# Two blocks in fp32 from split operands: new durations in the estimate that paces background steps, and two operand splits half a chunk earlier

## The chip, the cores and the metric

The kernel runs on one core of a Trainium2 chip. The metric is the time of one execution on the device in microseconds (us); "the median" is that over several executions.

## The reference

Two blocks follow each other on 256 tokens of 2048 features, in fp32. Cut to what matters here:

```python
# block 1
h = x @ w_in                                   # all inputs of four branches, and their gates
y_a = pool_mixer(...) * silu(a_gate);  y_b = spatial_gating(...) * silu(b_gate)
y_c = sliding_window_attention(...) * silu(c_gate);  y_d = conformer_conv(...) * silu(d_gate)
x = layer_norm(ALPHA * x + sum(sigmoid(g[i]) * (y[i] @ w_branch[i])) @ w_out)
# block 2
z, xbc, dt, q, k, v, f = split(rmsnorm(x) @ w_in_2)
y_ssd = rms(ssd(conv(xbc), dt) * silu(z))      # in two groups g of 512 features
y_fox = softmax(q k' / 8 + cum(f) - cum(f)') v # 16 heads of 64: "fox", causal
x = x + concat(y_ssd, y_fox) @ w_out_2
x = x + peer(rmsnorm(x))                       # top-k of keys, then 16384 experts: u, gelu, v
return rmsnorm(x)
```

## The kernel before, in words

**Stream.** Every weight passes through one stream of chunks of 128x2048 fp32 (1 MB, `load`, three buffers `wr`), and each chunk is worked in two halves. `split` (lines 283 to 303) makes of a half two fp32r operands: ACT casts `wh` from `wr` (a CAST), then DVE subtracts to give `wl`. TensorE multiplies three times per tile of 128 features: hi by hi, lo by hi, hi by lo; a half chunk is 24 matmuls of 256 columns (`T_chunk`) or 12 of 512 (`N_chunk`). There are four pairs of split buffers, and `split` is called three halves ahead (`LOOK`): the cast of half h+3 writes to the buffer that half h-1 used. Half chunks are counted from 0 below: the queries and keys of block 2 are halves 430 to 461 (one query or key tile of 128 features is two halves), its `z` 462 to 477, its `w_out_2` starts at 478.

**Background steps.** Everything between the large products (normalizations, both attentions, the SSD) is written as generators, "steps", in four lanes (`Tasks`, lines 62 to 160). After the third tile of each half chunk `bg()` calls `tasks.tick()`, which issues steps while the estimated clocks of DVE and ACT are less than 5 us ahead of PE's (`room`). The clocks are kept by `charge` from `Meter.cost` (lines 171 to 190), which is an estimate of each instruction's length: it decides nothing but which step is issued after which half chunk, that is, the order of the instructions on each engine. All PE, DVE and ACT instructions pass through `Meter` and so carry line 208.

**Where the order is forced.** `tasks.until` and `tasks.require` (lines 121 to 150) issue the steps of a named task at once, with no work of the stream between them. `ev_q2(j)` (line 1203) takes query tile j out of PSUM; there are two buffers for queries, so it first runs fox j-2 up to its last use of query j-2 (`until`). `pre_wout2` (line 1316) stands ahead of half 478: it evacuates `z`, requires fox 4 to 7, and casts and subtracts the fox outputs into XH and XL (`split_y`). `pre_yn(g)` (line 1329) requires the normalization of group g of the SSD for both token halves (`yn{g}0`, `yn{g}1`) and splits its result into XH and XL. At line 1344 a pair in place of one function names the first and the second half of a chunk.

A step of fox, of one block of 128 queries: two products K by q, scale and mask (DVE), row maximum; *then* two exponentials (ACT); *then* a reciprocal and two scalings (DVE); *then* transposes (PE, `bg<-cst,LS`) and a copy (ACT, `LS<-bg`); *then* the product with V (PE, `bg<-LS,VN`) and a copy to YF (ACT).

```python
def room(self):
    c = self.clock
    return max(c["dve"], c["act"]) < c["pe"] + HORIZON
def charge(self, eng, cost):
    lag = 0.0 if c.eng is None else 0.25 if c.eng != eng else 0.125 if eng == "dve" else 0.0
    t = max(self.clock[eng], c.t + lag) + cost
```

Of the kernel before, what the change touches and what calls it, by code (L numbers as in the profile page):

```python
# [7 lines left out]
FR = mybir.dt.float32r  # L8
U32 = mybir.dt.uint32
BF = mybir.dt.bfloat16  # L10
# [53 lines left out]
class Tasks:  # L64
# [83 lines left out]
    def charge(self, eng, cost):  # L148
        c = self.cur
        lag = 0.0 if c.eng is None else 0.25 if c.eng != eng else 0.125 if eng == "dve" else 0.0  # L150
        t = max(self.clock[eng], c.t + lag) + cost
        self.clock[eng] = t
        if c is not self.main:
            c.t, c.eng = t, eng


def size(ap):
    n = 1
    for d in ap.shape[1:]:
        n *= d  # L160
    return n
# [5 lines left out]
class Meter:  # L167
# [3 lines left out]
    def cost(self, name, out, a, k):  # L171
        n = size(out)
        if self.which == "pe":
            if name == "transpose":
                return n * 2 / 2400
            return n * (1 if a[1].dtype in (FR, BF) else 4) / 2400
        if self.which == "act":
            c = 0.04 + 0.89e-3 * n + (0.09 if k.get("accum_out") is not None else 0.0)
            f = TABLES.get(a[1]) if name == "activation" else None
            if f and f != self.tasks.table:  # L180
                self.tasks.table = f
                c += 1.28
            return c
        if name in ("bn_stats", "tensor_reduce", "max", "max_index"):
            n = size(a[-1 if name == "max_index" else 0])
        if name == "tensor_scalar" and not (hasattr(a[1], "shape") and hasattr(a[2], "shape")):
            return 0.1 + 0.6e-3 * n
        if name == "tensor_copy":
            return 0.1 + 0.6e-3 * n
        return (0.13 if name == "scalar_tensor_tensor" else 0.08) + 1.04e-3 * n  # L190

    def plain(self, name, out, a):
        n = size(out)
# [18 lines left out]
def kern(tc, A, out):  # L212
    nc = tc.nc
    with ExitStack() as ctx:
        ctx.enter_context(tc.manual_schedule())
        _kern(tc, nc, ctx, A, out)


def _kern(tc, nc, ctx, A, out):
    tasks = Tasks(4)  # L220
# [44 lines left out]
    def add_chunks(src, idxs, fns, cols=D, pres=None):  # L265
        for n, i in enumerate(idxs):
            stream.append((src[i], cols, fns[n], pres[n] if pres else None))
# [3 lines left out]
    def load(c):  # L271
        if c >= len(stream):
            return
        src, cols, _, _ = stream[c]
        t = wraw.tile([P, D], F32, name="wr")
        if c:
            nc.sync.dma_start(t[:, :cols], src)
        else:
            nc.sync.dma_start(t[:, :HALF], src[:, :HALF])
            load_x(1)  # L280
            nc.sync.dma_start(t[:, HALF:], src[:, HALF:])
        raws[c] = t

    def split(hc, eng=None):
        c, half = divmod(hc, 2)
        if c >= len(stream):
            return
        n = stream[c][1] // 2
        r = raws[c][:, half * n:half * n + n]
        h = wspl.tile([P, HALF], FR, name="wh")  # L290
        l = wspl.tile([P, HALF], FR, name="wl")
        SC.copy(h[:, :n], r)
        if stream[c][2] is state.get("dtf"):
            r, l = [x.rearrange("p (k n) -> p k n", k=8) for x in (r, h)]
            V.tensor_sub(l[:, :, 32:64], r[:, :, 32:64], l[:, :, :32].bitcast(F32))
        else:
            (eng or V).tensor_sub(l[:, :n], r, h[:, :n].bitcast(F32))
        splits[hc] = (h, l, max(tasks.clock["dve"], tasks.clock["act"]))
        if half:
            load(c + RAW_BUFS)  # L300
# [93 lines left out]
    def catch(upto, eng=None):  # L394
        while state["next"] <= upto:
            split(state["next"], eng)
            state["next"] += 1
# [923 lines left out]
    def split_y(g0, g1):  # L1321
        YS, YF = b2["YS"], b2["YF"]
        for g in range(g0, g1, 2):
            s = slice(g, g + 2)
            y = YS[:, s] if g < 8 else YF[:, g - 8:g - 6]
            SC.copy(XH[:, s], y)
            V.tensor_sub(XL[:, s], y, XH[:, s].bitcast(F32))

    def pre_yn(g):
        def f():  # L1330
            tasks.require(f"yn{g}0", f"yn{g}1")
            split_y(4 * g, 4 * g + 4)
        return f

    def ev_wout2(n):
        def f(t, ps):
            s = slice(n * 512, (n + 1) * 512)
            V.tensor_tensor(X[t][:, s], X[t][:, s], ps, op=OP.add)
            junk = b2["w"].tile([P, 512], F32, name="t2")
            SC.activation(junk, X[t][:, s], AF.Square, accum_out=small[:, 16 + 4 * t + n:17 + 4 * t + n])  # L1340
        return f

    evs = [ev_wout2(n) for n in range(4)]
    for n, kq, pre in [(0, 0, pre_wout2), (0, 1, (None, pre_yn(0))), (0, 2, None), (1, 0, None), (1, 1, None),
                       (1, 2, (None, pre_yn(1))), (0, 3, None), (1, 3, None)]:
        add_chunks(A["w_out2"], [4 * n + kq], [N_chunk(kq, evs[n], (2, 3, 0, 1), slot=n)], pres=[pre])
    for n in (2, 3):
        add_chunks(A["w_out2"], range(4 * n, 4 * n + 4),
# [348 lines left out]
    for hc in range(2 * len(stream)):  # L1697
        c, half = divmod(hc, 2)
# [4 lines left out]
        pre = stream[c][3]  # L1703
        if not isinstance(pre, tuple):
            pre = (pre, None)
# [126 lines left out]
```

## Time and profile before

| | us |
|---|---|
| three runs | 3096.13, 3102.93, 3100.11 |
| their median | 3100.11 |
| the profiled execution, its own time | 3101.19 |
| its span in the profile | 3099.5 |
| mean granted TensorE clock of it | 0.995 |

The profiled execution is 1.08 us above the median, and 1.7 us of its time lie around the span. The table of engines on the page gives busy time and its share of the span, then the number of instructions; PEld is the loading of weights into TensorE, which runs beside the matmuls. The granted clock is a share of full speed (1.00 is 2.4 GHz, 0.50 is 1.2 GHz). A row of the timeline gives start and length in us, engine, line, operation, output<-input and how many were merged; what stands in brackets is the idle time ahead of it and who ended it.

### The profile page before, as it was taken

The numbers are of one execution on the slowest core, as the hardware profiler recorded it, in microseconds if no ns is written. First come the engines' busy times: TensorE is split into PE (matmuls) and PEld (weight loads), VectorE is DVE, ScalarE is ACT, GpSimd is POOL, SyncE is SP. The second block draws the span as 40 slices with busy tenths as digits, with TensorE's granted clock in tenths as the row PEclk, the third lists the DMA queues.
The fourth block names the chain that finished last, engine by engine and source line by source line (L and its number), as shares of the span: only waits on it lengthen the run. The fifth ranks groups of instructions, "written<-read, shape, count | busy, mean of one in ns | idle before, by whom it ended". The sixth has DMA issues, their size and how long they took to land.

```text
span 3099.5 us, 53098 instructions
## 1 busy us (share of the span) xinstructions
PE 3053.1 (99%) x21964; PEld 2850.0 (92%) x21964; DVE 2200.7 (71%) x3195; ACT 1575.3 (51%) x2199; POOL 223.6 (7%) x187
## 2 busy tenths in 40 slices
PE   8999999999999989999999999999999999999998
PEld 8899999999999869897899999999999888888887
DVE  8899866555555567766489989788796666666665
ACT  4443565444444445556454457667675444444444
POOL 0000000000000020100000003233130000000000
PEclk9999999999999989999999999999999999999999
DMA  7555555555555535433545655666658766666654
GB/s 274 184 198 198 179 187 187 197 190 203 182 201 191 186 127 181 173 132 131 201 150 188 221 207 202 258 244 220 257 199 327 278 239 228 250 245 248 241 216 150
DMA packets 92226, 640.61 MB, mean 207 GB/s; under 512 B 10272, under 2 KB 10448, under 8 KB 17744
## 3 DMA queue, kind: packets, MB, share of 16 engines
q1 hardware_dynamic: 78192, 559.06, 49.9%
q0 software_dynamic: 13504, 77.63, 6.9%
q8 instruction: 172, 2.82, 0.4%
q14 instruction: 70, 0.57, 0.1%
q10 hardware_dynamic: 288, 0.52, 0.0%
HBM read 601.53 MB, written 35.65 MB: 206 GB/s over the span
## 4 chain that ended last, share of the span: by engine, by line
PE 96%; DVE 1%; ACT 1%; issue 1%; POOL 0%; DMA 0%; DVEq 0%; SPq 0%; ACTq 0%
PE pm L208 92%; PE bg L208 4%; ACT wh L208 1%; DVE wl L208 0%; DVE X L208 0%; DVE XL L208 0%; POOL keys L1516 0%; DMA wr<-w_in 0%; DVE stg L208 0%; ACT XH L208 0%; DVE gb L208 0%; DVE PX L208 0%; ACT PX L208 0%; ACT keys L208 0%; POOL Ad L1567 0%
## 5 line engine op out<-in xcount | busy, mean ns | idle before, releaser
L208 DVE TENSOR_TENSOR wl<-wr,wh 128x1024 fp32r<-128x1024 f32 x1048 | 1293.9, 1237 | 824.1 <-ACT wh L208 818.9
L208 ACT CAST wh<-wr 128x1024 fp32r<-128x1024 f32 x1054 | 1108.8, 1053 | 1383.5 <-PE pm L208 1325.8
L208 PE MATMUL pm<-XH,wh 128*128 128x256 f32 x4976 | 1393.7, 280 | 8.0 <-ACT wh L208 8.0
L208 PE MATMUL pm<-XL,wh 128*128 128x256 f32 x4976 | 1383.8, 278 | 0.0
L208 PE MATMUL pm<-XH,wl 128*128 128x256 f32 x4960 | 1380.4, 278 | 0.5 <-DVE wl L208 0.5
L208 PEld LDWEIGHTS pm<-XH,wh 128*128 128x128 f32 x4976 | 941.9, 189 | 14.1 <-ACT wh L208 8.0
L208 PEld LDWEIGHTS pm<-XL,wh 128*128 128x128 f32 x4976 | 937.5, 188 | 1.0 <-issue 0.7
L208 PEld LDWEIGHTS pm<-XH,wl 128*128 128x128 f32 x4960 | 932.7, 188 | 0.9 <-DVE wl L208 0.8
L208 PE MATMUL pm<-wh,whl 128*128 128x512 f32 x1024 | 398.3, 389 | 0.0
L208 PE MATMUL pm<-wh,whh 128*128 128x512 f32 x1024 | 398.3, 389 | 0.0
L208 PE MATMUL pm<-wl,whh 128*128 128x512 f32 x1024 | 398.3, 389 | 0.0
L208 PEld LDWEIGHTS pm<-wl,whh 128*128 128x128 f32 x1024 | 192.2, 188 | 39.9
L208 PEld LDWEIGHTS pm<-wh,whh 128*128 128x128 f32 x1024 | 192.2, 188 | 39.9
L208 PEld LDWEIGHTS pm<-wh,whl 128*128 128x128 f32 x1024 | 192.2, 188 | 39.8
L208 PE MATMUL pm<-wh,XH 128*128 128x512 f32 x448 | 179.5, 401 | 3.7 <-ACT XH L208 3.7
L208 PE MATMUL pm<-wh,XL 128*128 128x512 f32 x448 | 177.1, 395 | 0.7 <-DVE XL L208 0.7
L208 PE MATMUL pm<-wl,XH 128*128 128x512 f32 x448 | 177.7, 397 | 0.0
L1516 POOL TENSOR_TENSOR keys<-cst,t 128x512 f32<-128x512 f32 x64 | 137.1, 2142 | 207.1 <-ACT ga L208 206.9
L208 PE MATMUL pm<-YH,wh 128*128 128x256 f32 x512 | 144.1, 281 | 0.0
L208 PE MATMUL pm<-YL,wh 128*128 128x256 f32 x512 | 143.7, 281 | 0.0
L208 PE MATMUL pm<-YH,wl 128*128 128x256 f32 x512 | 143.7, 281 | 0.0
L208 DVE SCALAR_TENSOR_TENSOR CV<-R,par,CV 128x256 f32<-128x256 f32 x240 | 117.0, 487 | 7.3
(288 smaller groups left out, 2368.2 us busy)
## 6 DMA issues: line engine op xcount, KB each, us to landing
wr<-w_in SPq DMA_DIRECT2D x190, 1024.0 KB, 4.8
wr<-uT SPq DMA_DIRECT2D x128, 1024.0 KB, 4.9
wr<-v SPq DMA_DIRECT2D x128, 1024.0 KB, 4.9
wr<-w_branch SPq DMA_DIRECT2D x32, 1024.0 KB, 4.8
wr<-w_out SPq DMA_DIRECT2D x32, 1024.0 KB, 4.8
wr<-wq SPq DMA_DIRECT2D x16, 1024.0 KB, 4.8
Ad<-ast POOLq DMA_DIRECT2D x16, 1024.0 KB, 5.1
Gd<-stg POOLq DMA_DIRECT2D x16, 1024.0 KB, 11.8
```

Source lines behind the costliest of these rows:

```text
L208: return f(out, *a, **k)
L1516: G.tensor_tensor(x, it, t3[:, 0, n0:n0 + 4, None].to_broadcast([P, 4, P]), op=OP.subtract)
```

## The change

Two things. `Meter.cost` gets other constants (a matmul column 1/16 longer, ACT and DVE operations longer by 0.02 to 0.08 us and by 2 to 12% per element, accumulation on ACT 0.2 in place of 0.09), and in `split` DVE's subtraction is charged from ACT's clock + 0.25 on, where before it was charged as if it waited for nothing. And `pre_yn(0)` and `pre_yn(1)` stand ahead of the first half of their chunks (halves 480 and 488) where they stood ahead of the second.

```diff
-            return n * (1 if a[1].dtype in (FR, BF) else 4) / 2400
+            return n * (17 / 16 if a[1].dtype in (FR, BF) else 4) / 2400
         if self.which == "act":
-            c = 0.04 + 0.89e-3 * n + (0.09 if k.get("accum_out") is not None else 0.0)
+            c = 0.12 + 0.91e-3 * n + (0.2 if k.get("accum_out") is not None else 0.0)
...
         if name == "tensor_scalar" and not (hasattr(a[1], "shape") and hasattr(a[2], "shape")):
-            return 0.1 + 0.6e-3 * n
+            return 0.14 + 0.67e-3 * n
         if name == "tensor_copy":
-            return 0.1 + 0.6e-3 * n
-        return (0.13 if name == "scalar_tensor_tensor" else 0.08) + 1.04e-3 * n
+            return 0.14 + 0.67e-3 * n
+        return (0.15 if name == "scalar_tensor_tensor" else 0.1) + 1.1e-3 * n
...
+        at = tasks.main.t
         SC.copy(h[:, :n], r)
+        tasks.main.t = max(at, tasks.clock["act"] + 0.25)
...
             (eng or V).tensor_sub(l[:, :n], r, h[:, :n].bitcast(F32))
+        tasks.main.t = at
...
-    for n, kq, pre in [(0, 0, pre_wout2), (0, 1, (None, pre_yn(0))), (0, 2, None), (1, 0, None), (1, 1, None),
-                       (1, 2, (None, pre_yn(1))), (0, 3, None), (1, 3, None)]:
+    for n, kq, pre in [(0, 0, pre_wout2), (0, 1, pre_yn(0)), (0, 2, None), (1, 0, None), (1, 1, None),
+                       (1, 2, pre_yn(1)), (0, 3, None), (1, 3, None)]:
```

No instruction is added or removed. The order differs in halves 4 to 190 (block 1's projections) and 400 to 489 (block 2 up to its w_out_2); from half 490 on it is as before. Three places, in the rows of the instructions' order (names: `pm`, `bg` PSUM tiles, the number tells one tile from another; LS the scores of fox in two lanes; VN the values; t a sigmoid's output; xN merges equal instructions).

PE where query 2 of block 2 is evacuated, between halves 447 and 448, before:

```order
L208 MATMUL pm<-XL,wh 128x256
L208 MATMUL pm<-XH,wl 128x256
L208 MATMUL bg_14584<-K_12613,q_14208 128x256
L208 MATMUL pm<-K_12613,q_14208 128x256
L208 MATMUL pm<-XH,wh 128x256
```

and now:

```order
L208 MATMUL pm<-XL,wh 128x256
L208 MATMUL pm<-XH,wl 128x256
L208 MATMUL bg_14529<-cst,LS_12603 128x128 x2
L208 MATMUL bg_14533<-LS_12603,VN 64x128 x2
L208 MATMUL bg_14537<-K_12613,q_14184 128x256
L208 MATMUL pm<-K_12613,q_14184 128x256
L208 MATMUL pm<-XH,wh 128x256
```

The whole second part of fox 2's first block (transposes, product with V) and the K by q of its second block now stand between two matmuls of the stream, where only the K by q did. The same holds ahead of halves 452, 456 (fox 3, fox 4) and, without the exponentials, 460 (fox 5).

DVE at the same place, now:

```order
L208 TENSOR_SCALAR smf_14494<-smf_14494 128x2
L208 TENSOR_TENSOR PX<-PX,bg_14497 128x256
L208 TENSOR_TENSOR wl<-wr,wh 128x1024
L208 RECIPROCAL smf_14494<-smf_14494 128x2
L208 TENSOR_SCALAR LS_12603<-LS_12603,smf_14494 128x128 x2
```

The reciprocal and the scalings that those transposes read stand behind the `wl` of half 451, issued just ahead of them.

ACT at the start of w_out_2, ahead of half 478, now:

```order
L208 CAST wh<-wr 128x1024 x2
L208 ACT_TABLE_LOAD
L208 ACTIVATE t_15645<-pm 128x512
L208 ACTIVATE t_15648<-pm 128x512
L208 COPY LS_12603<-bg_15651 128x512
L208 COPY YF<-bg_15666 128x128
L208 ACT_TABLE_LOAD
L208 ACTIVATE LS_12604,smf_15663<-LS_12604,smf_15663 128x256 x2
L208 COPY LS_12604<-bg_15677 128x512
L208 COPY YF<-bg_15683 128x128
L208 CAST XH<-YF 128x512 x2
```

Before, the same `t` (sigmoids of z) were followed at once by `CAST XH<-YF`: fox 6 and fox 7 were done but for fox 7's last product with V. Now 3 steps of fox 6 and 6 of fox 7 are issued here with no matmul of the stream between them on PE.

ACT further on, from there to the splits of `pre_yn(0)`, before:

```order
L208 CAST XH<-YF 128x512 x2
L208 ACTIVATE PX,ss_15719<-PX 128x512
L208 ACT_TABLE_LOAD
L208 ACTIVATE ss_15719<-ss_15719,eps_81 128x1
L208 CAST wh<-wr 128x1024
L208 ACTIVATE PX,ss_15739<-PX 128x512
L208 ACTIVATE ss_15739<-ss_15739,eps_81 128x1
L208 CAST wh<-wr 128x1024 x2
L208 CAST XH<-XS 128x512 x2
```

and now:

```order
L208 CAST wh<-wr 128x1024 x2
L208 ACTIVATE XS<-bg_15748,par 128x128 x4
L208 CAST XH<-XS 128x512 x2
L208 CAST wh<-wr 128x1024
L208 ACTIVATE XS<-bg_15784,par 128x128 x4
```

`CAST XH<-XS` is the split of `pre_yn(0)`. It now stands half a chunk sooner, and the scaling of `yn01` (`XS<-bg_15748,par`) is forced right ahead of it.

## Rows read from the trace of the kernel before

**Rows 1.** The page: busy time, share of the span, instructions of each engine.

```profile
PE 3053.1 (99%) x21964; PEld 2850.0 (92%) x21964; DVE 2200.7 (71%) x3195; ACT 1575.3 (51%) x2199; POOL 223.6 (7%) x187
```

**Rows 2.** The page: share of each engine in the chain that ended last.

```profile
PE 96%; DVE 1%; ACT 1%; issue 1%; POOL 0%; DMA 0%; DVEq 0%; SPq 0%; ACTq 0%
```

**Rows 3.** PE's waits: who waited for whom: us in total, times, longest.

```profile
PE bg L208 <- issue: 9.5, 1, 9.5
PE pm L208 <- ACT wh L208: 8.0, 1, 8.0
PE bg L208 <- DVE diag L208: 7.2, 2, 5.0
```

**Rows 4.** Waits of all engines, the same columns.

```profile
ACT wh L208 <- PE pm L208: 1325.8, 910, 4.5
```

**Rows 5.** Chain that ended last: start, length, what, number of instructions.

```profile
208.31 8.48 PE pm L208 x72
217.24 8.18 PE pm L208 x72
...
512.49 617.34 PE pm L208 x4863
```

**Rows 6.** ACT and DVE timeline in the queries and keys of block 2.

```profile
1303.21 1.05 ACT L208 CAST wh<-wr 128x1024 fp32r<-128x1024 f32 x1 [2.00 <-PE pm L208]
...
1304.29 1.22 DVE L208 TENSOR_TENSOR wl<-wr,wh 128x1024 fp32r<-128x1024 f32 x1 [0.79 <-ACT wh L208]
...
1305.67 0.37 ACT L208 COPY LS<-bg 128x256 f32<-128x256 f32 x1 [1.14 <-PE bg L208]
```

**Rows 7.** DVE timeline at the end of z.

```profile
1448.30 0.16 DVE L208 RECIPROCAL smf<-smf 128x2 f32<-128x2 f32 x1
1448.49 0.62 DVE L208 TENSOR_SCALAR LS<-LS,smf 128x256 f32<-128x256 f32 x2
```

**Rows 8.** PE timeline at the end of z and in w_out_2: start, length.

```profile
1430.21 0.48 PE L208 MATMUL bg<-K,q 64*128 64x256 f32 x1
...
1441.38 0.99 PE L208 MATMUL bg<-cst,PX 128*128 128x128 f32 x4 [2.02 <-DVE PX L208]
...
1449.39 0.60 PE L208 MATMUL bg<-cst,LS 128*128 128x128 f32 x4
...
1470.27 0.79 PE L208 MATMUL pm<-wh,XH 128*128 128x512 f32 x1 [3.66 <-ACT XH L208]
1471.80 0.80 PE L208 MATMUL pm<-wh,XL 128*128 128x512 f32 x1 [0.74 <-DVE XL L208]
```

**Rows 9.** Stretches: us; PE, PEld, DVE, ACT, POOL busy (instructions); granted clock; DMA share; GB/s.

```profile
1347.00:1353.00 6.00, 5.11 (x48) 4.75 (x47) 5.12 (x12) 4.70 (x13) 1.43 (x2) 1.00 0.34 145
...
1441.00:1445.00 4.00, 3.62 (x11) 3.07 (x12) 1.46 (x2) 2.75 (x9) 0.00 (x0) 0.57 0.02 2
1469.00:1476.00 7.00, 4.99 (x12) 3.63 (x13) 5.60 (x9) 2.69 (x4) 0.00 (x0) 0.53 0.54 171
```

**Rows 10.** ACT timeline, end of z and w_out_2.

```profile
1432.67 0.25 ACT L208 COPY YF<-bg 128x128 f32<-128x128 f32 x1
...
1438.35 1.03 ACT L208 CAST wh<-wr 128x1024 fp32r<-128x1024 f32 x1
1439.40 1.28 ACT L208 ACT_TABLE_LOAD   x1
1440.69 0.51 ACT L208 ACTIVATE LS<-LS,smf 128x256 f32<-128x256 f32 x1
...
1451.24 0.60 ACT L208 COPY LS<-bg 128x512 f32<-128x512 f32 x1
...
1457.85 1.09 ACT L208 ACTIVATE t<-pm 128x512 f32<-128x512 f32 x2
...
1467.72 1.98 ACT L208 CAST wh<-wr 128x1024 fp32r<-128x1024 f32 x2
1469.60 1.13 ACT L208 CAST XH<-XS 128x512 fp32r<-128x512 f32 x2
```

## The prediction, made before the changed kernel ran

> **What bounds the kernel now.** I read the share of each engine first, then the chain that ended last, then PE's waits, then the timeline where the order changes. PE is busy 99% of the span, DVE 71% and ACT 51% [rows 1], and the chain that ended last is PE for 96% [rows 2]: the stream of matmuls sets the time, and a change in the order can gain only where PE waits. The three largest waits, 9.5, 8.0 and 7.2 us, are at the start of the program and at the boundary of the blocks [rows 3]; the change does not touch what they wait for. The cover of all background work is therefore nearly complete already. What gives it is the distance between split and use: ACT's casts wait 1325.8 us in total for PE to leave a buffer [rows 4], so each cast starts as soon as PE ends a half chunk, and PE has two more halves ready.
>
> PE itself has two speeds at the same granted clock. In the chain, 72 matmuls of the stream (three halves) take 8.48 us or 8.18 us, 117.8 or 113.6 ns each, and the pieces on either side of one group of background matmuls can differ so [rows 5]. The piece from 512.49 us on took 617.34 us for 4863 matmuls, of which 384 have 512 columns (the 32 half chunks of w_out, 12 each) and count double: 5247 units of 256 columns, 117.7 ns each. So the longest piece without background matmuls ran at the slower of the two [rows 5].
>
> **The change part by part.** No instruction is added or removed, and the longer estimates cost nothing by themselves. They make `room` close earlier, so that steps come later in the stream. That matters where a step is demanded at a fixed place: what is not done by then is issued there at once, with PE's stream behind it.
>
> *Four chains at the queries, halves 448, 452, 456, 460.* The order shows one step there before and five, five, five and four now: exponentials, reciprocal and scalings, transposes and copy, product with V, K by q. In front of them stand the cast and the subtraction of the half that is split at the same place. That cast can start only when PE is through with the half before [rows 4], so the chain starts when PE has nothing left: cast 1.05, `wl` 1.22, which covers the exponentials beside it, copy 0.37 [rows 6], reciprocal 0.16 and two scalings 0.62, taken from ones of 256 columns [rows 7]. The matmuls in it only move, so PE's idle time is 1.05 + 1.22 + 0.16 + 0.62 + 0.37 = 3.4 us in each. It sits between two matmuls of the stream, and nothing covers it.
>
> An idle PE can cost more after it. Where PE waited 2.02 us for PX [rows 8], the granted clock of the 4 us that follow was 0.57, between the levels of 2.4 GHz (1.00) and 1.2 GHz (0.50), with PE busy 3.62 us [rows 9]: 3.62 x 0.43 = 1.6 us lost. In 1347 to 1353 us PE idled 0.9 us in sum (6.00 less 5.11), and the clock stayed at 1.00 [rows 9]. A wait of 3.4 us is nearer the first, so I take 1.6 after each; the bounds are 0 and 2.3, the loss after a wait of 3.66 us: 4.99 busy us in 1469 to 1476 us at 0.53, 4.99 x 0.47 [rows 8, 9]. Four chains: 4 x (3.4 + 1.6) = +20.0; from 4 x 3.4 = 13.6 to 4 x (3.4 + 1.05 for another cast ahead + 2.3) = 27.
>
> *The chain ahead of w_out_2, half 478.* Nine steps of fox 6 and 7 are issued there. Off PE it holds one cast 1.05, a table load 1.28, two sigmoids 1.09, a copy of 512 columns 0.60, one to YF 0.25, a second table load 1.28 (the next function is an exponential), two exponentials of 0.51, [rows 10], reciprocal and scalings 0.78 [rows 7] and a copy 0.60: 7.95 us. Beside it PE does the first transposes, 0.60, and the K by q, 0.48 [rows 8]: 7.95 - 1.08 = 6.9 us idle. With 1.6 for the clock +8.5; bounds 6.9 and 10.2 (a further cast and 2.3).
>
> What a change of function costs is a row here: the cast before one ended at 1439.38, the load took 1.28 us and the exponential began at 1440.69 [rows 10], so nothing is drained around it. The Trainium skill, page "ScalarE: Activation LUTs", section "Table sets: the hidden batching unit", gives some 2.7 us for each load, drain included; by it two loads would make 2.8 us more, and the time 3123. The row speaks against it, and the sum goes by the row.
>
> *`pre_yn(0)` half a chunk sooner, half 480.* It forces two steps of `yn01`, transposes and scaling, which before had a half chunk, 2.7 us (a third of 8.18), of cover. The wait that I can compare is the one for the same XH at half 482, 3.66 us [rows 8]; the bounds are 0 and 3.7, and I take 1.5, since the products with the new XH come only half 482 and a half chunk of the stream lies between. For `pre_yn(1)` the normalization is done long before; nothing.
>
> *What is gained.* In before, XH for group 0 of the SSD is cast at 1469.60, behind two casts of the stream that begin at 1467.72 [rows 10]; PE waits 3.66 us for it and 0.74 for XL [rows 8], and loses 2.3 to the clock as above. Half a chunk sooner the split stands ahead of those casts. The 2.02 us at 1441.38, for PX, with its 1.6, falls as well, since those steps move. Together -(3.66 + 0.74 + 2.02 + 2.3 + 1.6) = -10.3; at the least -6.4, if the clock gives nothing.
>
> *POOL, SP and the DMAs.* A load is issued with the split of a second half, at the same place as before; POOL's mask sums move with their steps and are not in any of the chains. The halves 4 to 190 are reordered too: there DVE is the busiest beside PE, and I put 0 with 4 us to either side for pieces that change between the two speeds of PE.
>
> **Sum.** 20.0 + 8.5 + 1.5 - 10.3 = +19.7 us on the profiled execution's 3101.2: 3120.9. That execution is 1.1 us above the median of the runs, so 3120 against 3100.11. With the bounds of each term the forecast alone gives 3110 to 3130.
>
> **The rivals.** *(a) The same waits, but the long stretch at the faster speed.* Background matmuls of block 1 come later now, and the stretch without any starts some 500 matmuls later, after other groups. Which speed holds after the last group, the rows do not tell: it changes at some groups and not at others [rows 5]. At the fast speed the 4359 matmuls that remain (4743 units) gain 4743 x (117.7 - 113.6) = 19.4 us: 3120 - 19 = 3100. For it: both speeds are common. Against: before had the slow one there. It is decided by the length of a half chunk after 570 us. [...]
>
> *(b) Faster.* The waits at 1441 and 1470 us go, and the forced chains are hidden. This decides if PE still holds matmuls of the stream when the chain's cast begins; from a chain start 2.5 us earlier on, the four would cost under 1 us each and the whole under the 10.3 that is won. Time: 3100.1 - 10.3 = 3090. Against it: the cast waits for PE's last matmul of the half [rows 4], so there is nothing left to hide behind.
>
> *(c) The pacing moves nothing that counts*, since what PE waits for is set elsewhere [rows 3]: 3100 to 3101. Against it: the order shows the chains with no matmul between.
>
> *(d) Worse than the sum:* each chain also delays the casts behind it, so that PE waits for `wh` once more after each, another 1.05 for six places, and the slower speed spreads to 190 to 570 us (some 3300 units x 4.1 ns, 13 us at most): about 3140.
>
> **How the numbers follow.** A measurement of this kernel can tell 0.2%, 6.2 us, from no change: below 3093.9 is faster, above 3106.3 slower. Forecast 0.50, (a) 0.32, (b) 0.08, (c) 0.05, (d) 0.05. Slower: the forecast's 0.49, 0.06 of (a) (its chains at their upper bounds) and 0.05 of (d), 0.60. Faster: 0.07 of (a), chains at their lower bounds, and 0.07 of (b), 0.14. The rest, 0.26, is the same. The range takes in the forecast to near its upper bound and nearly all of (a): 3094 to 3129; outside lie (b), (d) and the ends of (a) and the forecast, 0.2.
>
> **What would show it.** Right: PE idles of 3 to 4 us ahead of halves 448, 452, 456 and 460 (about 1340 to 1400 us), released by LS; one or two of 7 us in sum near 1460 us; a granted clock under 1.00 behind each; no wait of 3.66 us for XH. The chain's piece from about 570 to 1130 us at 117.7 ns says forecast, at 113.6 rival (a). Wrong would be: full clock and no new idle at those places, or chains of which PE's waits are under 2 us.

## The result: 1.1% slower, just outside the range

The changed kernel takes 3132.38 us (median of four executions, 3130.28 to 3136.86); the kernel before, on the same chip, 3098.40. The ratio is 1.0110, 95% interval 1.0092 to 1.0127: 34 us slower, where 3120 (3094 to 3129) was forecast. The sign and the places were right, the sum too small. The profiled execution took 3130.28 us (span 3128.6), 29.1 us more than the one profiled before; the steps below are counted between these two. The other 4.9 us of the 34 are how the profiled executions lie to their medians (2.1 us below the one, 2.8 above the other), and no trace shows them.

The page of the changed kernel, busy time of each engine, and below it PE's waits in the trace (who waited for whom, us in total, times, longest):

```profile
PE 3063.8 (98%) x21964; PEld 2856.5 (91%) x21964; DVE 2206.5 (71%) x3195; ACT 1587.7 (51%) x2207; POOL 221.0 (7%) x187
```

```profile
PE bg L208 <- DVE diag L208: 16.9, 3, 9.5
PE bg L208 <- DVE LS L208: 14.5, 5, 3.4
PE pm L208 <- ACT wh L208: 8.1, 1, 8.1
PE bg L208 <- ACT LS L208: 7.1, 6, 4.5
...
PE bg L208 <- DVE PX L208: 1.8, 2, 1.6
```

The instructions of PE and DVE are as many as before [rows 1]; PE is busy 11 us more, some of it at a lower clock, DVE 6 and ACT 12 us. ACT has eight instructions more: its function sets change more often in the new order, 46 table loads where there were 38, at 1.28 us each. So the statement ahead of the forecast, and in it, that no instruction is added does not hold for these. New are 14.5 us for DVE's LS and 7.1 us for ACT's LS, the scores of fox; the wait of 3.7 us for XH at half 482 is gone, and one of 1.6 us for PX (the SSD's values on the way to their normalization) at half 480 is new. The `diag` waits at the boundary of the blocks now stand as 16.9 us; before, 9.5 of them were booked under `issue` [rows 3], at the same place. The first chain, ahead of half 448, in the timelines of ACT, DVE and PE:

```profile
1336.12 1.04 ACT L208 CAST wh<-wr 128x1024 fp32r<-128x1024 f32 x1 [4.14 <-PE pm L208]
...
1337.20 1.23 DVE L208 TENSOR_TENSOR wl<-wr,wh 128x1024 fp32r<-128x1024 f32 x1 [2.25 <-ACT wh L208]
...
1338.34 0.16 DVE L208 RECIPROCAL smf<-smf 128x2 f32<-128x2 f32 x1
...
1338.53 0.48 DVE L208 TENSOR_SCALAR LS<-LS,smf 128x128 f32<-128x128 f32 x2
...
1338.88 0.52 PE L208 MATMUL bg<-cst,LS 128*128 128x128 f32 x2 [2.73 <-DVE LS L208]
1339.44 0.37 ACT L208 COPY LS<-bg 128x256 f32<-128x256 f32 x1 [1.49 <-PE bg L208]
...
1339.86 0.69 PE L208 MATMUL bg<-LS,VN 128*64 128x128 f32 x4 [0.46 <-ACT LS L208]
...
1340.92 0.79 PE L208 MATMUL bg<-K,q 64*128 64x256 f32 x1 [0.36 <-ACT YF L208]
```

Read from the top: ACT's cast, which waited 4.14 us for PE to leave the buffer; DVE's `wl` behind it; the reciprocal and the scalings behind that; then PE's transposes, idle for 2.73 us, and two more waits of 0.46 and 0.36 us. In sum 3.55 us, as the forecast's chain of five terms had it (3.4). The stretches around the four chains, the chain ahead of half 478 and half 480 (us; PE, PEld, DVE, ACT, POOL busy; granted clock; DMA share; GB/s):

```profile
1335.00:1342.00 7.00, 3.44 (x20) 2.02 (x18) 1.78 (x4) 2.47 (x7) 0.00 (x0) 0.82 0.37 115
1342.00:1350.00 8.00, 8.00 (x57) 7.61 (x56) 3.03 (x7) 2.76 (x7) 0.00 (x0) 0.73 0.08 33
1357.00:1364.00 7.00, 3.25 (x17) 1.79 (x16) 3.78 (x11) 2.56 (x7) 0.00 (x0) 0.71 0.53 194
1364.00:1372.00 8.00, 8.00 (x61) 7.60 (x60) 3.33 (x7) 3.23 (x8) 0.00 (x0) 0.82 0.05 22
1380.00:1388.00 8.00, 4.44 (x23) 2.85 (x23) 3.92 (x12) 2.84 (x8) 0.00 (x0) 0.74 0.35 131
1388.00:1395.00 7.00, 7.00 (x52) 5.95 (x52) 2.05 (x5) 4.08 (x11) 1.44 (x2) 0.81 0.00 0
1402.00:1409.00 7.00, 3.44 (x21) 2.16 (x21) 2.27 (x6) 2.06 (x4) 0.00 (x0) 0.91 0.46 164
1409.00:1416.00 7.00, 7.00 (x55) 6.68 (x55) 2.92 (x5) 3.99 (x11) 0.00 (x0) 0.84 0.04 18
1470.00:1482.00 12.00, 3.44 (x22) 2.13 (x20) 5.95 (x11) 7.86 (x13) 0.00 (x0) 0.61 0.24 87
1482.00:1490.00 8.00, 8.00 (x30) 6.32 (x28) 2.60 (x5) 6.48 (x15) 0.00 (x0) 0.73 0.01 2
1490.00:1500.00 10.00, 8.17 (x42) 6.43 (x41) 6.59 (x12) 6.46 (x13) 0.00 (x0) 1.00 0.29 105
```

PE's missing time in the first of each pair is its idle time: 3.56, 3.75, 3.56 and 3.56 us at the queries, 8.56 us ahead of half 478, and 1.83 us at half 480. The clock is under 1.00 in both stretches of a pair; busy time by missing clock gives 0.6 + 2.2, 0.9 + 1.4, 1.2 + 1.3 and 0.3 + 1.1 us, 9.1 in sum, and 1.3 + 2.2 = 3.5 us at the fifth. These are estimates, since a row's clock is a mean over its whole stretch, idle time included: taken only where the clock stands at 0.50, half of PE's busy time there is 10.4 us at the four chains and 3.8 us at the fifth.

The longest waits of that fifth chain, in PE's timeline:

```profile
1474.71 1.12 PE L208 MATMUL bg<-LS,VN 128*64 128x128 f32 x8 [4.53 <-ACT LS L208]
1479.19 1.16 PE L208 MATMUL bg<-cst,LS 128*128 128x128 f32 x4 [3.36 <-DVE LS L208]
1481.03 1.12 PE L208 MATMUL bg<-LS,VN 128*64 128x128 f32 x8 [0.68 <-ACT LS L208]
```

The product with V of fox 6 waits 4.53 us for the copy behind casts, table load and sigmoids; fox 7's transposes wait 3.36 us for the exponentials and scalings behind a second table load.

**Where the 29.1 us went.** Idle in the four chains 14.4 and clock 9.1; the fifth chain 8.6 and 3.5; half 480 1.8; the waits of before that are gone -10.3 (the forecast's own sum): +27.1. Taken directly, from the first matmul of half 388 to that of half 490, the two traces differ by as much: 350.9 us before, 378.1 now. The start of half 388, before any of this, lies 2.3 us earlier than before (block 1's new order). The piece of the chain that starts at half 510 or so (2089 matmuls, the same in both) took 244.09 us against 238.53, +5.6; nothing shows that this is the change's (run 1, with the same kind of chains, has 238.53), see the last section. 27.1 - 2.3 + 5.6 = 30.4, so 1.3 us stay unexplained.

### The profile page after: what moved, and what is told of

The parts are those of the page before. It is cut to its first block, busy times and chain, and to the rows that moved or that the text cites. A ratio compares the mean times of both kernels' runs of the same rounds, so it can differ in the third digit from the quotient of the medians.

```text
span 3128.6 us, 53104 instructions
## 1 busy us (share of the span) xinstructions
PE 3063.8 (98%) x21964; PEld 2856.5 (91%) x21964; DVE 2206.5 (71%) x3195; ACT 1587.7 (51%) x2207; POOL 221.0 (7%) x187
## 4 chain that ended last, share of the span: by engine, by line
PE 96%; DVE 2%; ACT 1%; DMA 0%; issue 0%; SPq 0%; POOL 0%; DVEq 0%; ACTq 0%
PE pm L208 92%; PE bg L208 4%; DVE X L208 1%; ACT wh L208 1%; DVE wl L208 0%; DMA wr<-w_in 0%; DVE XL L208 0%; ACT LS L208 0%; ACT XH L208 0%; DVE cm L208 0%; ACT L208 0%; DVE LS L208 0%; SPq L436 0%; POOL keys L1519 0%; ACT XS L208 0%
```

## The experiments

Theory 1: the wait that `split` now charges on DVE makes every step's estimated end later, so that steps miss the tick of their half chunk, which comes once in 2.7 us, and are forced at the queries and at w_out_2. Theory 2: the longer lengths do it. Theory 3: the moved operand splits do it. In every run the ratio is to the kernel before on the same chip, whose median there was 3102 to 3103 us (in the result above 3098.40, of four executions), so that ratios compare better than times. Names in the waits below: XS the SSD's normalized output, ss its sums of squares, ZN z times its sigmoid, K a key tile, `diag` and `af` small DVE results.

**1. Only the wait in `split`.**

```diff
+        at = tasks.main.t
         SC.copy(h[:, :n], r)
+        tasks.main.t = max(at, tasks.clock["act"] + 0.25)
...
+        tasks.main.t = at
```

> Only the wait of DVE's half in split; old lengths, old place of the two operand splits. Theory 1 (the charged wait makes each step's estimated end later, steps miss the tick of their half chunk, and five to six of them are forced at halves 448, 452, 456, 460 and eight at 478): all of the loss and none of what the moved splits win, 3132 + 6, so 3130 to 3142, with the same idles of 3 to 4 us at the four places. Theory 2 (the longer lengths throttle the steps): within 6 us of 3098. Theory 3 (the moved operand splits cost the time): within 6 us of 3098.

Measured: 3132.89 us, ratio 1.0105 (1.0089 to 1.0122): the whole loss, by theory 1. Five and six steps are forced at the queries, eight at half 478, two at 481. PE's waits from 1325 to 1500 us in this trace:

```profile
PE bg L208 <- DVE LS L208: 12.7, 4, 4.5
PE bg L208 <- ACT LS L208: 10.8, 6, 8.3
PE bg L208 <- ACT YF L208: 1.5, 4, 0.4
PE pm L208 <- DVE ZN L208: 1.4, 1, 1.4
```

23.5 us for LS against 21.6 in the full change. The ratio is near that of the full change, where theory 1 would have had it 6 us above; but the intervals, some 5 us to either side, leave room for that, and from half 388 to half 490 this trace is 3.9 us longer (382.0 us against 378.1). What the moved splits win is left to run 3. With the splits in their old place, PE has no wait for XH, XL or PX here.

**2. Only the new lengths.** The constants of `Meter.cost` as in the change, all else as before.

> Only the new lengths. The order forces one step more at half 460 and two more at 478 than before. Theory 1: two short waits of 1 to 2 us each with little lost to the clock, 3098 to 3106. Theory 2: most of the 34 us, 3120 to 3135. Theory 3: 3098 within 6.

Measured: 3102.25 us, ratio 1.0006 (0.9995 to 1.0018). Theory 2 falls. The order does force two steps more at half 478, and PE waits there once:

```profile
1456.33 1.13 PE L208 MATMUL bg<-LS,VN 128*64 128x128 f32 x8 [3.35 <-ACT LS L208]
```

**3. Only the operand splits moved.** The two pairs `(None, pre_yn(g))` become `pre_yn(g)`.

> Only the two operand splits half a chunk sooner; estimate as before. Theory 1: the waits of 3.7 us for XH and 0.7 us for XL at half 482 and 2.3 us of clock behind them go, and up to 1.5 us is paid at half 480: 3090 to 3095. Theory 2 the same. Theory 3: 3105 or more, with a wait of over 4 us at half 480.

Measured: 3102.55 us, ratio 1.0000 (0.9990 to 1.0009). Theory 3 falls, and so does the forecast's reason for its gain. ACT and PE at half 482:

```profile
1465.40 1.28 ACT L208 ACT_TABLE_LOAD   x1
...
1466.90 1.04 ACT L208 CAST wh<-wr 128x1024 fp32r<-128x1024 f32 x1
...
1470.79 1.03 ACT L208 CAST wh<-wr 128x1024 fp32r<-128x1024 f32 x1
1471.72 1.13 ACT L208 CAST XH<-XS 128x512 fp32r<-128x512 f32 x2
...
1472.39 0.79 PE L208 MATMUL pm<-wh,XH 128*128 128x512 f32 x1 [2.72 <-ACT XH L208]
...
1473.73 0.79 PE L208 MATMUL pm<-wh,XL 128*128 128x512 f32 x1 [0.55 <-DVE XL L208]
...
1476.06 1.11 PE L208 MATMUL bg<-cst,PX 128*128 128x128 f32 x4 [1.11 <-DVE PX L208]
```

`CAST XH<-XS` now stands behind one cast of the stream where it stood behind two, and PE's wait is shorter by 0.94 us (2.72 against 3.66 [rows 8]). But ACT comes to it only at 1471.72, since the table loads, the squares and the casts ahead of it fill ACT; and PE then waits 1.11 us more for PX, the normalization of the other group. Half a chunk in the order was one microsecond on the engine, and that was paid elsewhere.

**4. SLACK 2.0 in place of -0.5**, in the changed kernel. A step is handed out when the estimate has its operands ready no later than `SLACK` after PE's clock, less 0.25.

```diff
-SLACK = -0.5
+SLACK = 2.0
```

> The changed kernel with SLACK 2.0 in place of -0.5: a step may be issued 2.5 us before the time at which the estimate has its operands ready. No step is forced then at the queries or at w_out_2. Theory 1: all chains go, the gains stay (10 us less waiting in block 2): 3085 to 3097, if PE does not wait at the steps instead. Theory 2: also faster than 3132, since lengths no longer matter. Theory 3: 3130 still. A rival of this run: PE waits at many steps in its own order, up to 2.5 us each, and the time stays above 3110.

Measured: 3098.42 us, ratio 0.9988 (0.9977 to 0.9999), 4 us below before, as theory 1 has it when counted from the 3098 that its range was made for; theory 3 and the rival fall. The full change, with the charged wait, the lengths and the moved splits, is no slower than before once steps may go out 2.5 us earlier: it is the rule of handing out together with the wait that costs, not the wait's being charged. By the first matmul of each half chunk in its trace it is 12.1 us behind the kernel before at half 424 and 2.1 us behind at half 490. Of the 12.1 us, 4.0 are there at half 50, where the orders hardly differ (the pitch of the last section), and 5.2 come between there and half 190, in block 1. So the next versions keep -0.5 in block 1.

**5. Idle filled with matmuls.** In the changed kernel, ahead of each round of forced steps, matmuls whose result nothing reads.

```diff
...
+            if self.filler:
+                self.filler(n)
...
+        def f(n):
+            for _ in range(counts[n] if n < len(counts) else 0):
+                nc.tensor.matmul(d[:, :S], h[:, :P], XH[:, 0], start=True, stop=True)
...
+                    tasks.filler = heat([12, 12, 4, 4] if j == 7 else [8, 8, 8, 4, 4])
...
+        tasks.filler = heat([0, 40, 15, 15, 6])
```

> The changed kernel with matmuls of no use (hi half by XH, 256 columns, result not read) ahead of the forced steps: 32 in each of the four chains at the queries, 76 in the one ahead of half 478, about as long as PE idled there. Theory A (an idle PE lowers the granted clock, and the matmuls behind pay for it): idle goes to nearly 0, the chains themselves are as long as before, the clock stays at 1.00, and the 2 to 3 us behind each of the four and 3.5 us behind the fifth come back: 3132 - 12, so 3117 to 3124. Theory B (the clock falls for another reason, or the time behind the chains is late steps): 3129 to 3137, clock under 1.00 as before.

Measured: 3122.49 us, ratio 1.0060 (1.0039 to 1.0081), 10 us less than the changed kernel with 204 matmuls more. The stretches of the first and the fifth chain, to be read against those of the changed kernel above (the first chain begins later here, at 1342 us, and so lies in the second row):

```profile
1335.00:1342.00 7.00, 7.00 (x62) 6.80 (x61) 5.26 (x11) 2.80 (x7) 1.57 (x2) 1.00 0.45 151
1342.00:1350.00 8.00, 8.00 (x64) 7.00 (x64) 3.39 (x8) 3.32 (x9) 0.00 (x0) 1.00 0.38 133
1470.00:1482.00 12.00, 12.00 (x99) 10.91 (x98) 6.91 (x14) 8.74 (x19) 0.00 (x0) 1.00 0.25 89
1482.00:1490.00 8.00, 5.15 (x23) 3.99 (x22) 3.73 (x6) 5.97 (x13) 0.00 (x0) 0.94 0.00 0
```

Theory A: PE is busy throughout, the clock is 1.00 in both chains, and most of what the clock had cost comes back. Behind the fifth a wait for PX of 2.8 us is left, and the clock falls once more behind it (0.94 here). How much comes back depends on the measure: 8.3 us by the traces from half 388 to half 490 (369.8 against 378.1), 10 us by the medians, some 14 by the distance of each to before on its own chip (20 and 34). So of the 34 us some 8 to 14 were clock and not waiting: shown by taking the idle away and leaving the chains as they were.

**6. SLACK 2.0 from block 2 on.**

```diff
+SLACK2 = 2.0
...
-                if first and not self.rate and self.lanes[i][2].t + 0.25 > self.clock["pe"] + SLACK:
+                if first and not self.rate and self.lanes[i][2].t + 0.25 > self.clock["pe"] + (SLACK if self.now < 388 else SLACK2):
```

> The changed kernel with SLACK 2.0 from half 388 on (block 2), -0.5 before. No step is forced. Theory 1: the chains go as with SLACK 2.0 everywhere, and block 1 stays as in the changed kernel, which reached half 190 some 3 us before the old one: 3085 to 3093. Rival: the 12 us that SLACK 2.0 everywhere won between halves 424 and 490 were only its own loss of 14 us ahead of them: 3096 to 3104.

Measured: 3095.95 us, ratio 0.9980 (0.9970 to 0.9990): faster than the kernel before by 6 us, the best of the versions measured. The expectations were made for 3098 before; against the 3102.24 of this chip the gain of 6.3 us lies at the lower edge of theory 1 and above what its rival allows. What PE still waits for in block 2 of it:

```profile
PE bg L209 <- DVE diag L209: 5.2, 1, 5.2
PE bg L209 <- DVE XS L209: 2.0, 2, 1.0
PE bg L209 <- ACT K L209: 1.8, 4, 0.9
PE pm L209 <- DVE XL L209: 1.0, 1, 1.0
```

No LS, no PX, no XH; half 490 begins 10.3 us earlier than before, and the 2089 matmuls behind it took 244.10 us, 5.6 us more than in before's trace, for the reason given in the last section.

**7. SLACK 2.0 at the queries only**, halves 388 to 461.

> SLACK 2.0 only in halves 388 to 461, -0.5 from z on. No step is forced at the queries; three of fox 7 at half 478 and two each of yn00 and yn01 at 480. Theory 1: the four chains, 23.5 us by the trace (14.4 idle, 9.1 clock), go, and the chain at 478 shrinks from nine steps to three, about 3 to 5 us: 3095 to 3106. Rival (the chain at the start of w_out_2 carries most of the loss): 3112 or more.

Measured: 3099.81 us, ratio 0.9992 (0.9980 to 1.0004), as theory 1 has it; the rival falls. With seven steps still forced at halves 478 and 480, PE waits there 3.3 us for ACT's LS and 1.4 us for ss. The chain at 478 shrank together with those at the queries, so this run doesn't part the two; the shares, 23.5 and 12.1 us, are the trace's.

**8. One group in the long stretch.** In the kernel before, ahead of half 200, four fp32 matmuls of 128 columns whose result nothing reads.

```diff
+FLIPS = (200,)
...
+        if hc in FLIPS:
+            p = pm.tile([P, 512], F32, name="pm")
+            for i in range(4):
+                nc.tensor.matmul(p[:, i * P:(i + 1) * P], ident, ident, start=True, stop=True)
```

> The kernel before with one group of four fp32 matmuls of 128 columns, result not read, ahead of half 200, in the stretch without background matmuls. If the pitch of the stream is a state that a group can turn: 113.5 in place of 117.7 ns from half 200 to 387, 3098 to 3103 less 18 us, so 3080 to 3086. If the long stretch is slow for a reason of its own: no change but 0.4 us for the group, within 5 us of before.

Measured: 3102.66 us, ratio 1.0000 (0.9989 to 1.0012). The stretch behind the group, from 620 us on, in this trace (same columns as above):

```profile
620.00:900.00 280.00, 280.00 (x2380) 280.00 (x2379) 151.15 (x176) 115.54 (x138) 0.53 (x1) 1.00 0.54 192
```

2380 matmuls in 280 us, 117.6 ns each, as in the changed kernel's trace (2380) and in that of before (2379). This one group didn't turn it, and no run here shows what would bring rival (a) about. Why this stretch is slow is open.

**9. The operand splits back in their old place**, in the version of 6.

> As the version with SLACK 2.0 from block 2 on, but with the two operand splits back in their old place, ahead of halves 481 and 489. If the earlier split matters once nothing is forced: a wait for XH or XL at half 482 of 2 to 4 us and some clock behind it, 0.9990 to 1.0005 of before (3099 to 3104 where before is at 3102). If what counts is only that the normalization is done by then: no new wait, 0.997 to 0.999 of before, as with the earlier split.

Measured: 3099.25 us, ratio 0.9991 (0.9980 to 1.0003), between the two expectations. Its interval overlaps that of 6. Half 482 waits a little more:

```profile
PE pm L209 <- DVE XL L209: 1.2, 1, 1.2
PE pm L209 <- ACT XH L209: 0.7, 1, 0.7
```

1.9 us for XH and XL against 1.0 us for XL alone. So the moved splits are worth about a microsecond by the trace (1.5 us from half 388 to half 490); whether by the time, these runs can't tell.

**10. SLACK 3.5 from block 2 on.**

> SLACK 3.5 in place of 2.0 from half 388 on. If steps handed out early make PE wait in its own order: more waits for LS, K and bg tiles between halves 400 and 477, 2 to 8 us in sum, 1.000 to 1.002 of before. If nothing waits for them: as SLACK 2.0, 0.997 to 0.999.

Measured: 3101.54 us, ratio 0.9993 (0.9982 to 1.0004), between the two expectations. In the trace PE waits for two things that it does not wait for at 2.0, PX 2.2 us and af 2.0 us: steps handed out too early now stand in PE's own order. From half 388 to half 490 its trace is 5.9 us longer than at 2.0 (349.2 against 343.3). The intervals for 2.0 and 3.5 overlap.

## Why the prediction fell short

- **What bounds the kernel**: right. PE's stream sets the time, and what the change cost is idle and clock of PE, at the places where the order stands still. The signs named in advance came: idle of 3.6 to 3.8 us ahead of the four halves, 8.6 us near 1475 us, a clock under 1.00 behind each.
- **The longer lengths cost nothing by themselves**: right for the time (run 2), but the forecast gave the later steps to "the longer estimates", and run 1 shows that the wait charged in `split` alone makes the chains. `room` was not what closed either: the rule in `tick` that a step's operands must be estimated ready 0.25 us + 0.5 us ahead of PE's clock is what holds steps back, for when it alone is relaxed, with `room` as it was, they go (runs 4 and 6).
- **Four chains at the queries**: the idle was right, 14.4 us against 13.6. The clock term failed, and it is the step that was wrong: "I take 1.6 after each", from the 4 us behind one wait of 2.02 us [rows 9]. Measured were 2.8, 2.4, 2.5 and 1.4 us, 9.1 against 6.4 (10.4 where the clock stands at 0.50). The row was read rightly, since the 7 us behind those 4 are at full clock again:

```profile
1445.00:1452.00 7.00, 7.00 (x36) 5.82 (x36) 4.90 (x9) 4.73 (x10) 0.00 (x0) 1.00 0.45 160
```

But it was the wrong row. "A wait of 3.4 us is nearer the first" holds against the 0.9 us of idle at full clock, not against the wait of 3.66 us, whose 2.3 us the forecast had and used as its bound: 4 x 2.3 = 9.2. Behind a chain the clock was 0.73 to 0.84 over the 7 or 8 us that follow, and the fp32 matmuls between the waits of a chain ran at the low clock too. Run 5 shows that it is idle that costs this.

- **The chain ahead of w_out_2**: the second term that was too small, 12.1 us against 8.5: idle 8.6 against 6.9, clock 3.5 against 1.6. In the idle, the forecast's 7.95 us of ACT and DVE were right within a microsecond; but of the 1.08 us that PE was to do beside them nearly all was done before the wait began, since the transposes and K by q stood ahead of it.
- **Half 480**: 1.8 against 1.5.
- **What is gained**: the size was right (the waits that the forecast summed to 10.3 us are gone), the reason was wrong. The forecast gave it to the earlier operand splits; run 3 shows that these alone win nothing, and in run 1, with the splits in their old place, the waits for XH, XL and PX are gone as well. That they are gone because PE stands still ahead of half 478 for 8.6 us, in which ACT and DVE catch up, is what the timelines suggest, and no run showed it by itself.
- **The table load**: 1.28 us in the chain again, without a gap (cast to 1471.79, load, sigmoids from 1473.09 in ACT's timeline). The Trainium skill, page "ScalarE: Activation LUTs", section "Table sets: the hidden batching unit", with its 2.7 us for a load would by estimate have made the sum 2.8 us larger, and nearer to the measured time, but for a reason that the trace doesn't have.
- **Rival (a)** had no part: the piece from 569.72 us on took 552.38 us for 4335 matmuls, and the windows show 117.6 ns each there (run 8). Of the others, (b) and (c) fall, since PE stood idle at the chains. Of (d), PE waits for `wh` once in the whole trace, 8.1 us, as it did before [rows 3], so the further waits that (d) gave each chain did not come; that its time, 3140, is nearer to 3132 than the forecast's 3120 is luck.
- **The range**: its upper end of 3129 left out part of what the terms' own upper ends allow: 27 + 10.2 + 3.7 - 6.4 = +34.5. The terms were not independent: the clock's cost was put too small in four of the five places at once. The profiled execution passed the forecast's 3120.9 by 9.4 us. The two chain terms make 7.1 of it and half 480 0.3; the rest is the pitch's +5.6, block 1's -2.3 and 1.3 unexplained. Without the pitch it would have lain near 3125, inside the range: that the time came out beyond it is in part the pitch, which nothing ties to the change.

## What to carry to other kernels

An estimate that paces background work is a dial, not a description: making one entry truer (the wait of a split) without retuning the rule that reads it (SLACK) forced 28 steps of fox into the stream at five places, where it had been four single ones, and cost 1.1%; with the rule moved by 2.5 us in block 2 the same estimate, with the moved splits, was 0.2% faster than before (with the splits in their old place the interval includes no change at all, run 9). Before moving a step earlier in the order, see how much earlier the engine reaches it: half a chunk in the order was one microsecond on a busy ACT. And price an idle of PE as the idle and the clock behind it, for the whole time that the clock is low: here 23.0 us of idle cost some 13 to 14 us more by the trace.

## What the runs showed of the hardware

The stream's pitch is not fixed by the program alone. The piece of 2089 matmuls from half 510 on is the same in all kernels here, and the chain that ended last shows it in one of two lengths; before's trace and that of the changed kernel (start, length, what, number):

```profile
1564.36 238.53 PE pm L208 x2089
```

```profile
1589.13 244.09 PE pm L208 x2089
```

Of the twelve traces eight show 238.5 to 239.0 us, four 244.1 to 244.6: 5.6 us apart with the same order, and the granted clock over the two pieces shown is 1.00. The first long piece differs so too between the trace of before and run 3, whose orders are equal up to half 478; before, then run 3:

```profile
9.21 181.10 PE pm L208 x1375
```

```profile
9.27 184.91 PE pm L208 x1375
```

The kernel before spreads over 3096 to 3111 us in all its executions, and such pieces are large enough to make a good part of that; that they make all of it was not shown. The longest stretch ran at the slow pitch in all twelve traces: from half 200 to half 356 each took 441.0 us, with the group added at its start too (run 8). What sets the pitch stays open.
